# A third pair of k tiles with seven products in place of eight, in a transformer block's large products

## The chip, the core and the metric

The kernel runs on one NeuronCore of a Trainium2 chip. Its engines run side by side, each with its own instruction list, in order: PE (the tensor engine; PEld is its weight load), DVE (vector), ACT (scalar), POOL (GpSimd) and SP (sync, which here only issues transfers). Data lies in HBM, is brought to SBUF by DMA, and PE writes its results to PSUM, eight banks of 128 x 512 float32. The metric is the device time of one execution in microseconds, the median of several runs.

## What is computed

One block of a streaming encoder on 256 tokens with a model width of 2048, in float32:

```python
def mixer_block(u, w_in, lb, hg_norm_w, rel_bias, w_branch_a, w_branch_b, w_out):
    z = u @ w_in
    hq, hf, hi, hg, aq, ak, av, gates = jnp.split(z, SPLIT_POINTS, axis=-1)
    ...
    gate_a, gate_b = jnp.split(jax.nn.sigmoid(gates), 2, axis=-1)
    merged = gate_a * (y_a @ w_branch_a) + gate_b * (y_b @ w_branch_b)
    return merged @ w_out

def reference(x, w_in, lb_logits, hg_norm_w, rel_bias, w_branch_a, w_branch_b, w_out,
              norm_mix_w, norm_mlp_w, w_up, w_down, norm_final_w):
    ...
        h = h + mixer_block(rms_norm(h, norm_mix_w[l]), w_in[l], lb_all[l], hg_norm_w[l],
                            rel_bias[l], w_branch_a[l], w_branch_b[l], w_out[l])
        u = rms_norm(h, norm_mlp_w[l])
        h = h + jnp.square(jax.nn.relu(u @ w_up[l])) @ w_down[l]
    return rms_norm(h, norm_final_w)
```

y_a is a gated linear recurrence, y_b an attention over chunks; both are left as they are. The large products are those with w_in (2048 x 11264), the branches (1024 x 2048 each), w_out (2048 x 2048), w_up (2048 x 8192) and w_down (8192 x 2048).

## The kernel before

**Products in three parts.** Each float32 operand is split into a rounded high part and a rest, `hi` and `lo` (`split`, L88): ACT copies to hi, DVE subtracts to get lo. A product of two 128-row tiles is then three matmuls with 512 columns (`mm3`, L142): hi with hi, hi with lo and lo with hi. The left side (256 tokens, so two row halves m = 0 and 1) is split once and stays in SBUF. The weights are streamed: a piece of 128 x 1024 values (512 KB), two k tiles of 512 columns, is loaded on SP's queue into a `raw` buffer (`piece`, L631) and split into a `wh` and a `wl` buffer (`parts`, L642). There are seven raw buffers and six pairs of wh and wl (`BUFS`, L621). A pool gives out a buffer when its last reader is done.

**Units.** `gemm_s` (L681) computes a unit: 256 rows by 1024 columns, n0 and n1 of 512 each, over 16 k tiles. There are 20 of them in the order ga2, gb0, gb2 (the gates' part of w_in), wo0, wo2 (w_out), then four times up and down: up00, up02, dn00, dn02, up10 and so on to dn30. The last 1024 columns of w_down in the fourth quarter are computed plainly by `gemm2` (L656), with the last four pieces of the last 512 columns held so that row half 0 ends before row half 1. Without savings a unit would have 16 x 2 x 2 = 64 products.

**Seven in place of eight.** A unit takes k tiles in pairs (k, k + 4). Such a pair is a 2 x 2 matrix of left tiles (row half by k tile) times a 2 x 2 matrix of weight tiles (k tile by column half), eight products. For the pairs (0, 4) and (1, 5) Winograd's form of Strassen's scheme is used, which needs seven products with sums on both sides. A product here spans both pairs, so it has 2 x 3 matmuls. `combos` (L586) makes the sums S2, S4, S5, S7 of the left side once for each left side and splits them; it is called seven times (x, m, h, and u in each quarter). The sums on the weight side are made by DVE in the raw buffers, `add` (L692), between the splits: four pieces 11, 22, 12, 21 are loaded, 22 += 12, 12 += 11, 11 += 22, 21 += 11, and each state of a piece is split when its product comes. The seven products p1 to p7 go into the four accumulators c11, c12, c21 and c22 (`bank`, six PSUM banks). c21 starts as ACT's copy of c11 (`copy`, L724); u1 and u2 are copies of c21 at two moments, subtracted in PSUM by DVE (`less`, L735). `fresh` makes PE write a bank once before ACT does, so that PE adds to it afterwards (`seeded`, L729).

**The other six pairs.** `plain` (L715) loads a piece of two neighbouring k tiles of one column half and multiplies it by both row halves, 12 matmuls. Two such pieces (k = 2 for each column half) are put between the seven products, partly as halves, to fill waits; ten follow. When the first column half is complete, `done` takes its banks away (sigmoid, squared relu, or an addition to h1); the last piece of the second half is left over (`late`) and is multiplied inside the next unit by `flush`. `between` is other work set in there: transposes of finished blocks (`turn`, `turns`, `h_blocks`), with their splits and `combos`.

**What sets the order.** The program is written in one sequence, and a scheduler places the instructions of each engine; splits, sums and copies are raised by `high_priority`. Within an engine's list nothing overtakes. Each transfer on SP waits for its raw buffer, in SP's order.

Of the kernel before, what the change touches and what calls it, by code (L numbers as in the profile page):

```python
# [16 lines left out]
P = 128  # L17
T = 256
# [32 lines left out]
def tile_hybrid_block(  # L51
# [36 lines left out]
    def split(hi, lo, src, copy=None):  # L88
        (copy or nc.scalar.copy)(hi, src)  # L89
        nc.vector.tensor_tensor(lo, src, hi.bitcast(F32), op=ALU.subtract)  # L90
# [130 lines left out]
    def rows(factors, what):  # L221

        wide = small.tile([P, NM, P], F32, name=f"wide_{what}", tag="wide", bufs=2)
# [124 lines left out]
    def hgrn_scores(n, kk, b, q):  # L348
# [11 lines left out]
        for i, B in enumerate(LEVELS):  # L360
# [10 lines left out]
            rr = small.tile([P, npar, 4], F32, name=f"rr{n}_{B}", tag=f"rr{B}", bufs=2)  # L371
# [130 lines left out]
    TOK = 18  # L502
# [82 lines left out]

    def combos(lhs, what, home):  # L586

        full = []
        for j in range(2):
            f = tk.tile([P, 2, T], F32, name=f"full_{what}{j}", tag="t", bufs=TOK)  # L590
            nc.vector.tensor_tensor(f, lhs[j][:, :2, 0, :].bitcast(F32), lhs[j][:, :2, 1, :].bitcast(F32), op=ALU.add)
            full.append(f)
        a11, a21 = full[0][:, :, :P], full[0][:, :, P:]
        a12, a22 = full[1][:, :, :P], full[1][:, :, P:]
        made = {}
        s = {i: tk.tile([P, 2, P], F32, name=f"s{i}_{what}", tag="t", bufs=TOK) for i in (5, 2, 4, 7)}
        nc.vector.tensor_tensor(s[5], a21, a22, op=ALU.subtract)
        nc.vector.tensor_tensor(s[2], s[5], a11, op=ALU.subtract)
        nc.vector.tensor_tensor(s[4], a12, s[2], op=ALU.add)
        nc.vector.tensor_tensor(s[7], a11, a21, op=ALU.subtract)  # L600
        for i in (4, 2, 7, 5):
            t = (tk if home == "a" else xp).tile([P, 2, 2, P], F32R, name=f"S{i}_{what}", tag=f"S{i}{home}", bufs=1)
            split(t[:, :, 0, :], t[:, :, 1, :], s[i])
            made[i] = t
        return made
# [15 lines left out]
    BUFS = {"raw": (6, 1), "wh": (4, 2), "wl": (4, 2)}  # L621
# [9 lines left out]
    def piece(w, n0, kt, what):  # L631

        raw = buf("raw", F32, what)
        if w.shape[-1] < NC:
            nb = NC // T
            src = w[n0 // T:n0 // T + nb, kt // 8, :, kt % 8:kt % 8 + 2, :].rearrange("c p a n -> p c a n")
            nc.sync.dma_start(raw.rearrange("p (c a n) -> p c a n", c=nb, n=T), src)
        else:
            nc.sync.dma_start(raw.rearrange("p (a n) -> p a n", n=NC), w[n0 // NC, kt // 4, :, kt % 4:kt % 4 + 2, :])
        return raw  # L640

    def parts(raw, w, what):  # L642

        made = [buf(t, F32R, what) for t in ("wh", "wl")]
        dst, src = made, raw
        if w.shape[-1] < NC:
            dst = [t.rearrange("p (a c n) -> p a c n", a=2, n=T) for t in made]
            src = raw.rearrange("p (c a n) -> p a c n", a=2, n=T)
        with tc.high_priority(offset=2000):
# [6 lines left out]
    def gemm2(lhs, w, n0, nkt, what, kt0=0, tail=0):  # L656

        acc = [bank(f"{what}{m}") for m in range(NM)]
        held = []

        def mm(m, k, wh, wl):
            for a in range(2):
                mm3(acc[m], *lhs_of(lhs, k + a, m), wh[:, a], wl[:, a], k + a == 0, k + a == nkt - 1)

        for k in range(0, nkt, 2):
            ps = (k, *parts(piece(w, n0, kt0 + k, f"{what}{k}"), w, f"{what}{k}"))
            if k >= nkt - tail:
                held.append(ps)
                continue
            for m in range(NM):  # L670
                mm(m, *ps)
        for m in range(NM):
            for ps in held:
                mm(m, *ps)
        return acc
# [5 lines left out]
    def gemm_s(lhs, S, w, n0, what, done, kt0=0, between=None, fresh=()):  # L681
# [6 lines left out]
        B = {}  # L688
        for i, (n, k) in {"11": (n0, 0), "22": (n1, 4), "12": (n1, 0), "21": (n0, 4)}.items():
            B[i] = piece(w, n, kt0 + k, f"{what}{i}")  # L690

        def add(dst, b):  # L692
            with tc.high_priority(offset=2000):
                nc.vector.tensor_tensor(B[dst], B[dst], B[b], op=ALU.add)  # L694

        def product(i, lh, src, n):

            wh, wl = parts(B[src], w, f"{what}{n}")

            def mm():  # L700
                first = i not in c
                if first:
                    c[i] = bank(f"{what}c{i}")
                for a in range(2):
                    mm3(c[i], *lh(a), wh[:, a], wl[:, a], first and a == 0, False)

            return mm
# [7 lines left out]
        def plain(k, n):  # L715
            wh, wl = parts(piece(w, n0 + n * NC, kt0 + k, f"{what}r{n}_{k}"), w, f"{what}r{n}_{k}")

            def mm(m):
                for a in range(2):
                    mm3(c["12"[m] + "12"[n]], *lhs_of(lhs, k + a, m), wh[:, a], wl[:, a], False, k + a == KD - 1)  # L720

            return mm
# [6 lines left out]
        def seeded(i):  # L729

            c[i] = bank(f"{what}c{i}")
            if i in fresh:
                nc.tensor.matmul(c[i], lhs[0][:, 0, 0, 0:P], lhs[0][:, 0].rearrange("p u t -> p (u t)"), start=True, stop=False, skip_group_check=True)

        def less(dst, i, t):  # L735
            with tc.high_priority(offset=2000):
                nc.vector.tensor_tensor(c[dst], c[i], t, op=ALU.subtract)

        p1 = product("11", of(0, 0), "11", "p1")
        p3 = product("12", comb(4), "22", "p3")  # L740
        add("22", "12")
        add("12", "11")
        p1()
        seeded("21")
        copy(c["21"], "11")
        product("22", comb(5), "12", "p5")()
        flush()
        add("11", "22")
        product("21", comb(2), "11", "p6")()
        u1 = copy(token(f"u1_{what}"), "21")  # L750
        seeded("12")
        less("12", "22", u1)
        product("11", of(0, 1), "21", "p2")()
        ps = plain(2, 0)
        ps(0)
        p3()
        product("21", comb(7), "22", "p7")()
        add("21", "11")
        u2 = copy(token(f"u2_{what}"), "21")
        pq = plain(2, 1)  # L760
        pq(0)
        pq(1)
        product("21", of(1, 1), "21", "p4")()
        less("22", "22", u2)
        ps(1)
        if between:
            between()
        def both(n, *ks):
            for k in ks:
                ps = plain(k, n)  # L770
                ps(0)
                ps(1)
# [5 lines left out]
        both(0, 6, 8)  # L778
        both(1, 6, 8)
        both(0, 10, 12, 14)  # L780
        end(0)
        both(1, 10, 12)

        def rest():
            both(1, 14)
            end(1)
# [10 lines left out]
    for gates, c, col, what, fresh in ((ga, 2, C_GA, "ga", ("21", "12")), (gb, 0, C_GB, "gb", ("21",)), (gb, 2, C_GB, "gb", ())):  # L797
# [56 lines left out]
    for n0 in (0, 2):  # L854
# [5 lines left out]
        gemm_s(mT, Sm, w_out, n0 * NC, f"wo{n0}", lambda m, n, acc, n0=n0: evict(h1[n0 + n][m], acc),  # L860
# [7 lines left out]
    for qd in range(NQ):  # L868
# [23 lines left out]
        for c in range(0, 4, 2):  # L892
# [11 lines left out]
            gemm_s(hT, Sh, w_up, qd * (FF // NQ) + c * NC, f"up{qd}{c}", done, between=turns)  # L904
# [26 lines left out]
        for n0 in (0, 2):  # L931
            if not (last and n0):
                gemm_s(uT, Su, w_down, n0 * NC, f"dn{qd}{n0}", lambda m, n, acc, n0=n0: out_of(m, n0 + n, acc), kt0=qd * KD,
                       between=None if n0 else turns)
                continue
# [48 lines left out]
```

## Time and profile before

| | us |
|---|---|
| median of three runs | 1450.09 (1448.04 to 1452.49) |
| the profiled execution, its own time | 1450.73 |
| its span, first to last instruction | 1449.0 |
| mean granted clock of PE | 0.995 of full speed |

In the profile a group of instructions has its line, engine, operation, the tiles written and read, the shape and the count, then busy time, mean ns of one, and the idle time before with what ended it. A row of the timeline begins with start and duration in us. wh_up20p is a buffer of unit up20 for a product p1 to p7, wh_up20r one for a plain piece. A matmul's row lasts longer than the time to the next one's start, as matmuls are pipelined; its cost is read from the starts.

### The profile page before, as it was taken

Reading aid. Unit: us, or ns where it says so; the run is one execution under the profiler, and the core shown is the slowest. Engines: PE = TensorE matmul, PEld = TensorE weight load, DVE = VectorE, ACT = ScalarE, POOL = GpSimd, SP = SyncE. Lnnn points to the kernel's source line nnn. Section 1 sums busy time; section 2 is a strip of 40 time slices with the busy share of each in tenths; the row PEclk is TensorE's granted clock in tenths of the full one; section 3 lists DMA queues with packets and bytes.
Section 4 is the critical chain, followed back from the end, with each engine's and each line's share of the span. In section 5 each row is a group of like instructions: output and inputs, shape, how many; then the busy total and the mean of one; then the engine's idle time right before and its main releaser. Section 6 shows DMA issues by size and latency. Waiting matters only on the chain.

```text
span 1449.0 us, 18212 instructions
## 1 busy us (share of the span) xinstructions
PE 1427.1 (98%) x6741; PEld 1185.2 (82%) x6741; DVE 1047.8 (72%) x1364; ACT 807.3 (56%) x1040; POOL 34.5 (2%) x96
## 2 busy tenths in 40 slices
PE   9999999999999999999999999999999999999997
PEld 7878888888787888888888887888888887888886
DVE  7797978565657774677887876778776868677753
ACT  6755844464555554445666654566545665456642
POOL 2000001010000000000000000000000000000000
PEclk9999999999999999999999999999999999999999
DMA  9644554646456656666655566555557645666551
GB/s 323 218 158 143 161 172 133 195 127 194 143 180 212 216 187 205 195 198 218 204 189 167 170 201 228 190 187 171 183 204 233 203 152 182 216 209 229 196 182 59
DMA packets 106089, 272.87 MB, mean 188 GB/s; under 512 B 8960, under 2 KB 9728, under 8 KB 105616
## 3 DMA queue, kind: packets, MB, share of 16 engines
q1 hardware_dynamic: 103264, 264.80, 55.5%
q0 software_dynamic: 1584, 5.31, 1.4%
q10 hardware_dynamic: 1152, 1.60, 0.3%
q8 instruction: 53, 0.87, 0.2%
q14 instruction: 36, 0.29, 0.1%
HBM read 269.57 MB, written 2.10 MB: 187 GB/s over the span
## 4 chain that ended last, share of the span: by engine, by line
PE 93%; DVE 3%; ACT 2%; issue 1%; DMA 1%; POOL 0%; SPq 0%; POOLq 0%; ACTq 0%
PE acc_hq L171 2%; PE acc_ak L171 2%; PE acc_aq L171 2%; PE acc_hf L171 2%; PE ps L395 1%; PE acc_bb L145 1%; PE acc_bb L143 1%; PE acc_ba L145 1%; PE acc_av L145 1%; PE acc_bb L144 1%; PE acc_ba L144 1%; PE acc_av L143 1%; PE acc_ba L143 1%; PE acc_av L144 1%; PE acc_dn02c L143 1%; PE acc_up22c L143 1%
## 5 line engine op out<-in xcount | busy, mean ns | idle before, releaser
L171 PE MATMUL acc_hf<-act_x,wh_hf 128*128 128x512 f32 x128 | 47.8, 409 | 0.2
L171 PE MATMUL acc_aq<-act_x,wh_aq 128*128 128x512 f32 x128 | 47.9, 407 | 0.0
L171 PE MATMUL acc_hq<-act_x,wh_hq 128*128 128x512 f32 x128 | 45.9, 398 | 0.0
L171 PE MATMUL acc_ak<-act_x,wh_ak 128*128 128x512 f32 x128 | 44.8, 396 | 0.0
L694 DVE TENSOR_TENSOR raw_up<-raw_up,raw_up 128x1024 f32<-128x1024 f32 x32 | 39.2, 1224 | 1.0
L170 PE MATMUL acc_aq<-act_x,wl_aq 128*128 128x256 f32 x120 | 35.2, 294 | 0.0
L694 DVE TENSOR_TENSOR raw_dn<-raw_dn,raw_dn 128x1024 f32<-128x1024 f32 x28 | 34.3, 1224 | 0.9
L170 PE MATMUL acc_hf<-act_x,wl_hf 128*128 128x256 f32 x120 | 34.4, 287 | 0.0
L90 DVE TENSOR_TENSOR wl_ga<-raw_ga,wh_ga 128x1024 fp32r<-128x1024 f32 x16 | 19.6, 1225 | 19.5 <-ACT wh_ga L89 19.5
L170 PE MATMUL acc_ak<-act_x,wl_ak 128*128 128x256 f32 x120 | 33.5, 279 | 0.0
L170 PE MATMUL acc_hq<-act_x,wl_hq 128*128 128x256 f32 x120 | 33.5, 279 | 0.0
L90 DVE TENSOR_TENSOR wl_av<-raw_av,wh_av 128x1024 fp32r<-128x1024 f32 x16 | 19.6, 1225 | 18.1 <-ACT wh_av L89 18.1
L90 DVE TENSOR_TENSOR wl_dn<-raw_dn,wh_dn 128x1024 fp32r<-128x1024 f32 x16 | 19.6, 1226 | 16.7 <-ACT wh_dn L89 16.7
L90 DVE TENSOR_TENSOR wl_ba<-raw_ba,wh_ba 128x1024 fp32r<-128x1024 f32 x16 | 19.6, 1225 | 16.5 <-ACT wh_ba L89 16.3
L90 DVE TENSOR_TENSOR wl_bb<-raw_bb,wh_bb 128x1024 fp32r<-128x1024 f32 x16 | 19.6, 1224 | 16.0 <-ACT wh_bb L89 16.0
L89 ACT CAST wh_bb<-raw_bb 128x1024 fp32r<-128x1024 f32 x16 | 16.9, 1056 | 23.5 <-PE acc_ba L145 12.7
L89 ACT CAST wh_dn<-raw_dn 128x1024 fp32r<-128x1024 f32 x16 | 16.9, 1056 | 23.0 <-PE acc_dn L145 13.3
L89 ACT CAST wh_ba<-raw_ba 128x1024 fp32r<-128x1024 f32 x16 | 16.9, 1055 | 22.6 <-PE acc_ba L145 10.0
L89 ACT CAST wh_av<-raw_av 128x1024 fp32r<-128x1024 f32 x16 | 16.9, 1056 | 22.0 <-PE acc_av L145 12.3
L171 PEld LDWEIGHTS acc_hf<-act_x,wh_hf 128*128 128x128 f32 x128 | 24.3, 190 | 5.6 <-DVE wh_hf L89 0.3
L89 ACT CAST wh_aq<-raw_aq 128x1024 fp32r<-128x1024 f32 x16 | 16.8, 1052 | 21.4 <-PE acc_aq L171 8.1
L171 PEld LDWEIGHTS acc_hq<-act_x,wh_hq 128*128 128x128 f32 x128 | 24.3, 190 | 5.4
(840 smaller groups left out, 5026.2 us busy)
## 6 DMA issues: line engine op xcount, KB each, us to landing
raw_dn<-in_w_down_dram SPq DMA_DIRECT2D x44, 512.0 KB, 5.4
raw_up<-in_w_up_dram SPq DMA_DIRECT2D x32, 512.0 KB, 5.2
raw_ga<-in_w_in_t_dram SPq DMA_DIRECT2D x20, 512.0 KB, 4.5
raw_hi<-in_w_in_n_dram SPq DMA_DIRECT2D x16, 512.0 KB, 4.5
raw_hg<-in_w_in_n_dram SPq DMA_DIRECT2D x16, 512.0 KB, 3.6
raw_aq<-in_w_in_t_dram SPq DMA_DIRECT2D x16, 512.0 KB, 4.4
raw_ak<-in_w_in_t_dram SPq DMA_DIRECT2D x16, 512.0 KB, 4.1
raw_av<-in_w_in_n_dram SPq DMA_DIRECT2D x16, 512.0 KB, 4.2
```

The source lines that it names most:

```text
L89: (copy or nc.scalar.copy)(hi, src)
L90: nc.vector.tensor_tensor(lo, src, hi.bitcast(F32), op=ALU.subtract)
L143: nc.tensor.matmul(acc, hi, wh, start=first, stop=False, skip_group_check=True)
L144: nc.tensor.matmul(acc, hi, wl, start=False, stop=False, skip_group_check=True)
L145: nc.tensor.matmul(acc, lo, wh, start=False, stop=last, skip_group_check=True)
L170: nc.tensor.matmul(acc[:, cb, 0:T], wl[:, c], r[:, 0, :], start=False, stop=False)
L171: nc.tensor.matmul(acc[:, cb, :], wh[:, c], r.rearrange("p u t -> p (u t)"), start=kt == 0, stop=kt == nkt - 1)
L395: nc.tensor.matmul(ps[:, m, :], klf[:, a * P:(a + 1) * P], qrf[:, a * 192:(a + 1) * 192], start=True, stop=True)
L694: nc.vector.tensor_tensor(B[dst], B[dst], B[b], op=ALU.add)
```

## The change

- Three pairs, (0, 4), (1, 5) and (2, 6), are now done with seven products; k tiles 3 and 7 become the first plain piece of each column half. `combos` uses 384 columns in place of 256 and adds hi and lo by row half; S5, S7, S2 and S4 are made in place.
- The third pair's four weight tiles come as two pieces of mixed halves: X holds tiles 11 and 22 of that pair, Y tiles 21 and 12. `piece` takes two halves and issues two transfers of 256 KB where they are not neighbours. The sums on X and Y are made on halves (128 x 512); X is split twice, Y once and its first half once more.
- In wo2 and up00 only two pairs are done so (`r=2`). All other units, and the last one of w_down, which is now a `gemm_s` with `tail`, take three: 18 and that one.
- A split piece is multiplied as soon as its turn comes: p3 is no longer held back, and the two plain pieces with it are used as halves around p7 and p4. Bank 12 now gets p3 directly, and DVE adds a copy of bank 22 (s5) and takes u1 off later.
- Buffers: eight raw in place of seven, 17 tokens (128 x 512) in place of 18, and small tiles of the recurrence moved to another pool.

```diff
 def combos(lhs, what, home):
-    for j in range(2):
-        f = tk.tile([P, 2, T], F32, name=f"full_{what}{j}", tag="t", bufs=TOK)
-        nc.vector.tensor_tensor(f, lhs[j][:, :2, 0, :].bitcast(F32), lhs[j][:, :2, 1, :].bitcast(F32), op=ALU.add)
...
+    for m in range(NM):
+        for j in range(2):
+            t = tk.tile([P, R, P], F32, name=f"a{m}{j}_{what}", tag="t", bufs=TOK)
+            x = lhs[j][:, :R, :, m * P:(m + 1) * P].bitcast(F32)
+            nc.vector.tensor_tensor(t, x[:, :, 0, :], x[:, :, 1, :], op=ALU.add)
...
-    BUFS = {"raw": (6, 1), "wh": (4, 2), "wl": (4, 2)}
+    BUFS = {"raw": (6, 2), "wh": (4, 2), "wl": (4, 2)}
...
+    def piece(w, what, *halves):
+        raw = buf("raw", F32, what)
...
+        for i, (n, k) in enumerate(halves):
+            nc.sync.dma_start(raw[:, i * NC:(i + 1) * NC].rearrange("p (c n) -> p c n", n=ncols),
+                              w[n // ncols:(n + NC) // ncols, k // kpr, :, k % kpr, :].rearrange("c p n -> p c n"))
+        return raw, False
...
+    def gemm_s(lhs, S, w, n0, what, done, r=R, kt0=0, between=None, fresh=False, tail=False):
+        W11 = load("11", (n0, 0), (n0, 1))
+        if r == 3:
+            X = load("x", (n0, 2), (n1, 6))
+        W22 = load("22", (n1, 4), (n1, 5))
+        W12 = load("12", (n1, 0), (n1, 1))
+        if r == 3:
+            Y = load("y", (n0, 6), (n1, 2))
+        W21 = load("21", (n0, 4), (n0, 5))
...
+        p = parts(W11, f"{what}p1")
+        if r == 3:
+            px = parts(X, f"{what}px")
+        mm("11", of(0, 0), p, *both)
+        if r == 3:
+            mm("11", of(0, 0), px, (0, 2))
+        c["21"] = bank(f"{what}c21")
...
+        copy(c["21"], "11")
+        p = parts(W22, f"{what}p3")
+        add(W22[0], W12[0])
+        add(W12[0], W11[0])
+        mm("12", comb(4), p, *both)
+        if r == 3:
+            mm("12", comb(4), px, (1, 2))
+        p = parts(W12, f"{what}p5")
+        mm("22", comb(5), p, *both)
+        if r == 3:
+            add(half(X, 1), half(Y, 1))
+            add(half(Y, 1), half(X, 0))
+            py = parts(Y, f"{what}py")
+            mm("22", comb(5), py, (1, 2))
+        more("12", copy(token(f"s5_{what}"), "22"), ALU.add)
+        if r == 3:
+            mm("11", of(0, 1), py, (0, 2))
+        p = parts(W21, f"{what}p2")
+        mm("11", of(0, 1), p, *both)
+        add(W11[0], W22[0])
+        flush()
+        p = parts(W11, f"{what}p6")
+        mm("21", comb(2), p, *both)
+        if r == 3:
+            add(half(X, 0), half(X, 1))
+            px = parts(X, f"{what}px2")
+            mm("21", comb(2), px, (0, 2))
+        u1 = copy(token(f"u1_{what}"), "21")
...
+        left = [(k, k + 1) for k in range(2, KD, 2) if k != 4] if r == 2 else [(3, 7)] + [(k, k + 1) for k in range(8, KD, 2)]
+        q1 = plain(1, *left[0])
+        q1(1)
+        more("12", u1, ALU.subtract)
+        p = parts(W22, f"{what}p7")
+        mm("21", comb(7), p, *both)
+        if r == 3:
+            mm("21", comb(7), px, (1, 2))
+        u2 = copy(token(f"u2_{what}"), "21")
+        q1(0)
+        add(W21[0], W11[0])
+        q0 = plain(0, *left[0])
+        q0(0)
+        more("22", u2, ALU.subtract)
+        p = parts(W21, f"{what}p4")
+        mm("21", of(1, 1), p, *both)
+        if r == 3:
+            add(half(Y, 0), half(X, 0))
+            mm("21", of(1, 1), parts(Y, f"{what}p4y", 0), (0, 2))
+        q0(1)
...
+        plains(0, *left[1:-3])
+        plains(1, *left[1:-3])
+        plains(0, *left[-3:])
+        end(0)
+        if tail:
+            held = [plain(1, *ks) for ks in left[-3:]]
+            for m in range(NM):
+                for p in held:
+                    p(m)
+                done(m, 1, c["12"[m] + "2"])
+            return
+        plains(1, *left[-3:-1])
...
-    gemm_s(hT, Sh, w_up, qd * (FF // NQ) + c * NC, f"up{qd}{c}", done, between=turns)
+    gemm_s(hT, Sh, w_up, qd * (FF // NQ) + c * NC, f"up{qd}{c}", done, r=R if qd or c else 2, between=turns)
...
     for n0 in (0, 2):
-        if not (last and n0):
-            gemm_s(uT, Su, w_down, n0 * NC, f"dn{qd}{n0}", lambda m, n, acc, n0=n0: out_of(m, n0 + n, acc), kt0=qd * KD,
-                   between=None if n0 else turns)
-            continue
-        flush()
-        for n in (2, 3):
-            for m, acc in enumerate(gemm2(uT, w_down, n * NC, KD, f"dn{qd}{n}", kt0=qd * KD, tail=8 if n == 3 else 0)):
-                out_of(m, n, acc)
+        gemm_s(uT, Su, w_down, n0 * NC, f"dn{qd}{n0}", lambda m, n, acc, n0=n0: out_of(m, n0 + n, acc), kt0=qd * KD,
+               between=None if n0 else turns, tail=last and n0 == 2)
```

`mm(i, lh, ps, *tiles)` multiplies the named tiles of a split piece into bank i, three matmuls each; `more` adds to or subtracts from a bank in PSUM on DVE; `half(W, i)` is one 512-column half of a raw piece; `plain(n, *ks)` loads and splits a plain piece and returns a function that multiplies it by one row half.

More of the change, by code (lines that the diff above doesn't have):

```diff
@@ L679, in evict, with add, mm @@
             nc.vector.tensor_tensor(dst, acc, dst, op=ALU.add)
-    def gemm_s(lhs, S, w, n0, what, done, kt0=0, between=None, fresh=()):
+    def gemm_s(lhs, S, w, n0, what, done, r=R, kt0=0, between=None, fresh=False, tail=False):
         n1 = n0 + NC
         c = {}
[L688 to L692, printed above, removed]
-            with tc.high_priority(offset=2000):
[L694 to L707, printed above, removed]
+        load = lambda name, *halves: piece(w, f"{what}{name}", *[(n, kt0 + k) for n, k in halves])
+        W11 = load("11", (n0, 0), (n0, 1))
[6 more added lines that the diff above has]
+        W21 = load("21", (n0, 4), (n0, 5))
+        def add(dst, t):
+            with tc.high_priority(offset=2000):
+                nc.vector.tensor_tensor(dst, dst, t, op=ALU.add)
+        half = lambda W, i: W[0][:, i * NC:(i + 1) * NC]
+        def mm(i, lh, ps, *tiles):
+            first = i not in c
+            if first:
+                c[i] = bank(f"{what}c{i}")
+            wh, wl = ps
+            for a, k in tiles:
+                mm3(c[i], *lh(k), wh[:, a], wl[:, a], first, False)
+                first = False
         def of(m, jj):
@@ L713, in comb @@
             return lambda k: [S[i][:, k, u, :] for u in range(2)]
[L715 to L722, printed above, removed]
+        both = ((0, 0), (1, 1))
         def copy(dst, i):
@@ L759, in gemm_s, with more @@
-        u2 = copy(token(f"u2_{what}"), "21")
[L760 to L765, printed above, removed]
+        def more(i, t, op):
+            with tc.high_priority(offset=2000):
+                nc.vector.tensor_tensor(c[i], c[i], t, op=op)
+        p = parts(W11, f"{what}p1")
[4 more added lines that the diff above has]
+            mm("11", of(0, 0), px, (0, 2))
```

123 lines of the change are left out of this document (50 added, 73 removed).

## The prediction

> **What bounds the kernel now.** I read the page first, then the waits of PE (the tensor engine), then its timeline, then the windows of four units in a row.
>
> ```profile
> span 1449.0 us, 18212 instructions
> PE 1427.1 (98%) x6741; PEld 1185.2 (82%) x6741; DVE 1047.8 (72%) x1364; ACT 807.3 (56%) x1040; POOL 34.5 (2%) x96
> PEclk9999999999999999999999999999999999999999
> PE 93%; DVE 3%; ACT 2%; issue 1%; DMA 1%; POOL 0%; SPq 0%; POOLq 0%; ACTq 0%
> ```
>
> PE is busy for 98% of the span at full granted clock, and the chain that ended last is 93% PE. What PE lost in waiting is little:
>
> ```profile
> PE ps L395 <- DVE sd L357: 3.3, 3, 2.9
> PE acc_dn02c L143 <- ACT wh_dn02r L89: 1.8, 1, 1.8
> PE acc_ga2c L143 <- ACT acc_ga2c L726: 0.6, 1, 0.6
> PE acc_dn20c L143 <- ACT act_u L89: 0.5, 1, 0.5
> ```
>
> Only about 3 us of it lie in the units that change. So a matmul that is left out is worth its spacing, as long as the others still come without a gap. The spacing is read from starts, because the 0.39 us of a row overlaps the next one. Between these two rows of PE's timeline lie 72 steps:
>
> ```profile
> 899.79 0.39 PE L145 MATMUL acc_dn02c<-wh_dn02r,act_u 128*128 128x512 f32 x1
> 916.12 0.39 PE L145 MATMUL acc_dn02c<-wh_dn02r,act_u 128*128 128x512 f32 x1
> ```
>
> (916.12 − 899.79) / 72 = 0.2268 us. A unit of 186 matmuls takes 42.2 us. The windows show how full the others are meanwhile (columns: length, PE, PEld, DVE, ACT, POOL, PE's clock, DMA share, GB/s; the four are up20, up22, dn20 and dn22):
>
> ```profile
> 1089.00:1131.00 42.00, 42.00 (x187) 34.75 (x186) 30.00 (x27) 23.52 (x26) 0.00 (x0) 1.00 0.63 205
> 1131.00:1175.00 44.00, 44.00 (x202) 36.18 (x201) 35.20 (x40) 29.11 (x38) 0.00 (x0) 1.00 0.59 190
> 1175.00:1221.00 46.00, 45.49 (x206) 36.43 (x205) 32.65 (x32) 25.45 (x30) 0.00 (x0) 1.00 0.57 182
> 1221.00:1263.00 42.00, 42.00 (x187) 34.75 (x187) 30.89 (x29) 21.32 (x22) 0.58 (x1) 1.00 0.58 198
> ```
>
> DVE (vector) has 9 to 13 us free in a unit, ACT (scalar) 15 or more, and the DMA engines are busy 0.6 of the time (the last share of a row).
>
> **The change part by part.** *Matmuls.* A product is three matmuls. One product less in 18 units is 54; w_down's last unit goes from two plain halves to the seven-product form and loses three products, 9; of the three seeding matmuls at ga2 and gb0 two remain, 1. That is 64, and the two instruction lists differ by just that number. 64 × 0.2268 = 14.5 us off PE. The Trainium skill, TensorE: Matmul & The Clock Gate, section "Wait — 56ns, not 53.3ns?", measures 215.7 ns between warm matmuls of 512 columns; by that the term would be 13.8 us; here the measured spacing is 226.8 ns, and it decides.
>
> *Work added on DVE and ACT.* Prices:
>
> ```profile
> L694 DVE TENSOR_TENSOR raw_up<-raw_up,raw_up 128x1024 f32<-128x1024 f32 x32 | 39.2, 1224 | 1.0
> L90 DVE TENSOR_TENSOR wl_up20r<-raw_up20r,wh_up20r 128x1024 fp32r<-128x1024 f32 x12 | 14.7, 1224 | 6.9 <-ACT wh_up20r L89 6.7
> L591 DVE TENSOR_TENSOR full_u<-act_u x8: 691/693/693, 805.3 to 1328.9; 128x512 f32<-128x512 f32 x8
> L90 DVE TENSOR_TENSOR S_u<-s_u,S_u x16: 416/418/421, 811.9 to 1335.6; 128x256 fp32r<-128x256 f32 x16
> L737 DVE TENSOR_TENSOR acc_up20c<-acc_up20c,u_up x2: 696/698/700, 1097.4 to 1104.2; 128x512 f32<-128x512 f32 x2
> L89 ACT CAST wh_up20r<-raw_up20r 128x1024 fp32r<-128x1024 f32 x12 | 12.7, 1056 | 8.4 <-PE acc_up20c L145 8.4
> L726 ACT COPY u_up<-acc_up20c x2: 590/590/590, 1096.0 to 1101.5; 128x512 f32<-128x512 f32 x2
> ```
>
> A changed unit gets 1.5 more splits (px, py and a second px come in place of two plain ones, and the half split p4y), four half adds and one more correction of a bank (s5). On DVE: 1.5 × 1.22 + 4 × 0.69 + 0.70 = 5.3 us; on ACT: 1.5 × 1.06 + 0.59 = 2.2 us. The combinations of the left side grow from 256 to 384 columns; no row has that shape on DVE, so it lies between 0.42 and 0.69, and I take the middle, 0.56: about 2 us for each of the seven. up20 comes to 35 of 41.5 us, up22 to 42.5 of 43.3. Recorded times overlap, though:
>
> ```profile
> 1085.43 1.22 DVE L90 TENSOR_TENSOR wl_up20p<-raw_up,wh_up20p 128x1024 fp32r<-128x1024 f32 x1
> 1086.57 1.22 DVE L90 TENSOR_TENSOR wl_dn12r<-raw_dn12r,wh_dn12r 128x1024 fp32r<-128x1024 f32 x1
> 1122.86 3.74 DVE L694 TENSOR_TENSOR raw_up<-raw_up,raw_up 128x1024 f32<-128x1024 f32 x3
> ```
>
> Splits in a row start 1.14 us apart; adds that need each other take 3.74 / 3 = 1.25. So DVE's real need in up22 is some 38 us. On the mean it is hidden behind PE; the question is the burst. The seven products with their plain companions are 99 matmuls, 22.5 us of PE, and DVE has about 28 us of work for them, 4 us of it evictions and corrections. The missing 6 us have to be done ahead, and six split buffers allow that: the plain part leaves DVE 2.7 − 1.1 = 1.6 us per piece.
>
> I laid out one unit by hand, up20, with t = 0 where PE begins p1, in the order in which the changed kernel's lists stand. PE wants p6 after 48 matmuls, t = 10.9; p7 after 63, t = 14.3; bank 12 again (first use of the (3,7) piece there) after 72, t = 16.3. DVE can start p3's split at −5.7: its buffer falls free three plain pieces before t = 0, at −8.2, ACT's copy and one eviction follow. From p3 to p6 it has six splits, four full adds and an eviction, 6 × 1.14 + 4 × 1.25 + 0.6 = 12.4, so p6 is ready at 6.7: 4 us early. Then come the two tight places:
>
> 1. ACT copies bank 21 (u1) between p6 and p7. Before, 18 matmuls (4.1 us) lay between them; now only the 6 of one half of the (3,7) piece, 1.36 us. The copy in the trace starts 0.2 to 0.3 us behind PE and takes 0.59: done 0.8 to 0.9 after p6, 0.5 us to spare, if ACT is free.
> 2. ACT is in order, and ahead of that copy stand the copies for the second (3,7) piece and for p4. That piece's transfer can start only when p6's split has freed its raw buffer, t = 6.7, as two transfers of 256 KB. How long transfers take (two views, of tiles loaded by w_up and by w_down):
>
> ```profile
> 1096.03 0.59 ACT L726 COPY u_up<-acc_up20c 128x512 f32<-128x512 f32 x1 [0.26 <-PE acc_up20c L145]
> 1096.52 1.06 ACT L89 CAST wh_up20p<-raw_up 128x1024 fp32r<-128x1024 f32 x1
> 1097.47 1.05 ACT L89 CAST wh_up20r<-raw_up20r 128x1024 fp32r<-128x1024 f32 x1
> DMA to landing us min/median/max: 3.7/4.7/5.3
> DMA to landing us min/median/max: 3.5/4.6/6.3
> ```
>
> It lands at 6.7 + 3.7 to 4.7 = 10.4 to 11.4; two ACT copies 0.95 apart and u1 end at 13.7 (u1 by PE) to 13.9; wanted 14.3. DVE then has the (3,7) split, an eviction, p4 and the correction of bank 12: ready at 15.2 to 16.1, wanted 16.3. So nothing to half a microsecond is left, and units that carry more before p6 (dn20 with the combinations of u, wo2 and up00 with those of h) will miss it. Bounds per unit: 0 at a landing of 3.7; at 6.3, 13.0 + 1.9 + 0.6 − 14.3 = 1.2 us late. I take 0.15, near the median's end, as not every unit is late: 19 × 0.15 = 3 us.
>
> *Transfers.* 76 loads of 512 KB become 152 of 256 KB, the same bytes, all on SP's queue, which only issues; X and Y stand there ahead of W22 and W21 and wait for older buffers, but all four are wanted more than 5 us after landing. One more raw buffer, one token less, and the factor tiles in another pool: nothing, no load or copy of the hand layout waits for them; without that cover one copy of 0.6 us.
>
> *The end.* The two row halves of the last bank are now 18 matmuls apart, 4.1 us, where it was 24.
>
> ```profile
> 1434.44 0.69 DVE L679 TENSOR_TENSOR h<-acc_dn,h 128x512 f32<-128x512 f32 x1 [8.52 <-PE acc_dn L145]
> 1436.98 1.34 ACT L928 ACTIVATE h<-h,rstd 128x512 f32<-128x512 f32 x2 [1.08 <-POOL rstd L96]
> ```
>
> The first half's chain lasts 1438.32 − 1434.44 = 3.9 us, so it still ends before the second needs ACT: 0, at most 0.5.
>
> **Sum.** 1449.0 − 14.5 + 3 = 1437.5 of span. That execution took 1450.73, 1.7 more than its span and 0.6 above the median of 1450.09. So 1439.2 for its like, and 1438.6 as a median. The old waits in ga2, dn02 and dn20 may go too (−3), which I leave to the range.
>
> **The rivals.**
> - *Bursts on DVE decide.* If its lead shrinks below what the hand layout shows, PE waits for splits in the units with turns and combinations, eleven of the 21. For it: up22's need of 38 to 42.5 us in 43.3. Against: the same units ran before at 35.2 of 44 with no wait. At 1 us each: 1438.6 + 11 = 1450.
> - *The second (3,7) transfer lands late; slower.* The place is p7 waiting for u1 behind ACT's copy of that piece. It decides from 14.5 / 19 = 0.76 us per unit on, a landing of 5.9 us. For it: the maxima of 5.3 and 6.3 above, and that the piece shares the queue with two others issued in the 5 us before it. Against: the median of 4.7. At a whole 7 us, the price is 13.7 + 2.5 − 14.3 = 1.9 a unit, 36 us, 1472; at 6.1, 1.0 a unit, 1455. By DMA: Bandwidth & Descriptors of the Trainium skill, section "Anatomy of one DMA", a transfer costs some 2.0 us plus its bytes at 436 GB/s, an estimate of 2.6 for each half and 5.2 if the halves followed each other, where the whole one would need 3.2; at 5.2 a unit would be 0.1 late. The shortest landing here of a whole one is 3.5.
> - *The change saves nothing on PE*, because the matmuls left out are made up by others: excluded by the lists but for a slip of mine; 1450.
>
> **How the numbers follow.** Forecast 0.63: 1438.6, own range 1434 to 1445. DVE bursts 0.16: 1446 to 1453. Late transfer 0.18: 1450 to 1470, mostly near 1456. No saving 0.03. The range reaches from 1433.5 (all waits gone, 14.5 + 2 off) to 1455. What a measurement can tell from no change is 0.3%, 4.4 us: faster means below 1445.7, slower above 1454.5. Faster: 0.62 of the first, 0.04 of the second, 0.02 of the third: 0.68. Slower: 0.03 and 0.13: 0.16 and a little for what I do not see, 0.19. Same: 0.13.
>
> **What would show it.** PE should have 64 matmuls fewer at 0.2268 us and still 98%; DVE some 1170 us busy, ACT some 860. In the waits of PE, a line with p7's bank 21 waiting for ACT's u, or bank 12 for DVE's correction, totals under 5 us if I am right and over 14 if the second rival is; waits for wl tiles would be the first. A higher spacing of the matmuls, or waits at places that I did not lay out (gates, w_out), would make me wrong in another way.

## The result, and the profile after

| | before | after |
|---|---|---|
| median, us | 1449.8 (4 runs) | 1461.63 (1460.13 to 1462.88, 4 runs) |
| ratio to before | | 1.008, 95% interval 1.0061 to 1.0098 |
| span of the profiled execution | 1449.0 | 1460.1 |
| span less PE's busy time | 21.9 | 24.4 |

The forecast was 1438.6 with 1455 as the upper end; the change made the kernel slower, by 0.8%. The page of the kernel after:

```profile
span 1460.1 us, 18523 instructions
...
PE 1435.7 (98%) x6677; PEld 1175.4 (81%) x6677; DVE 1151.5 (79%) x1522; ACT 847.3 (58%) x1105; POOL 34.7 (2%) x96
...
PEclk9999999999999999999999999999999999999999
...
PE 81%; DVE 8%; DMA 4%; ACT 3%; issue 2%; SPq 0%; POOL 0%; POOLq 0%; ACTq 0%; DVEq 0%
```

PE executes the 64 matmuls fewer that were counted, 6677 against 6741, at full granted clock, and yet it is busy 8.6 us longer. So the loss isn't in waits first of all. The waits of PE in the units (engine and tile, who released it, us in total, times, the longest):

```profile
PE acc_gb0c L143 <- ACT u_gb L726: 1.6, 1, 1.6
PE acc_ga2c L143 <- ACT wh_ga2p L89: 1.4, 1, 1.4
...
PE acc_dn20c L143 <- ACT u_dn L726: 0.9, 1, 0.9
PE acc_dn32c L143 <- ACT u_dn L726: 0.8, 1, 0.8
...
PE acc_dn10c L143 <- ACT u_dn L726: 0.5, 1, 0.5
PE acc_dn30c L143 <- ACT u_dn L726: 0.4, 1, 0.4
```

The copy u holds PE up for 4.2 us in all, where the "late transfer" rival needed over 14; span less busy grew by only 2.5. What grew is the step from one matmul to the next. Two rows of PE's timeline, 72 steps apart in the plain part of the same unit as in the prediction:

```profile
904.61 0.39 PE L143 MATMUL acc_dn02c<-wh_dn02r,act_u 128*128 128x512 f32 x1
...
921.34 0.39 PE L143 MATMUL acc_dn02c<-wh_dn02r,act_u 128*128 128x512 f32 x1
```

(921.34 − 904.61) / 72 = 0.2324 us, where it was 0.2268. The step grew in stages that the change doesn't touch, too. Here are rows of the branch products 72 steps apart, first of the kernel before, then of the kernel after:

```profile
565.43 0.39 PE L143 MATMUL acc_ba<-wh_ba,act_ya 128*128 128x512 f32 x1
...
581.75 0.39 PE L143 MATMUL acc_bb<-wh_bb,act_yb 128*128 128x512 f32 x1
```

```profile
571.39 0.39 PE L143 MATMUL acc_ba<-wh_ba,act_ya 128*128 128x512 f32 x1
...
588.11 0.40 PE L143 MATMUL acc_bb<-wh_bb,act_yb 128*128 128x512 f32 x1
```

That is 0.2267 us before and 0.2322 after, in code that is the same in both. Rows of unit up20 show that it isn't so for all matmuls. The operands behind the arrow are the moving weight tile and the stationary left tile; S_h is a combination, act_h a plain left tile:

```profile
1110.02 0.39 PE L143 MATMUL acc_up20c<-wh_up20p,S_h 128*128 128x512 f32 x1
...
1111.83 0.40 PE L145 MATMUL acc_up20c<-wh_up20px,S_h 128*128 128x512 f32 x1
...
1115.51 0.40 PE L143 MATMUL acc_up20c<-wh_up20r,act_h 128*128 128x512 f32 x1
...
1118.07 0.39 PE L145 MATMUL acc_up20c<-wh_up20r,act_h 128*128 128x512 f32 x1
```

Eight steps with S take 1.81 us, 0.2263 each; eleven with act take 2.56, 0.2327 each. Shape, type, clock and the pools of the moving buffers are the same.

The compiled kernels' addresses give the difference. The tiles of the pool small lie ahead of the weight buffers in SBUF. With the factor tiles wide and rr gone from it, the weight buffers behind it moved down by 4736 bytes per partition, 18 × 256 + 128:

| first byte modulo 256 | act | wh, wl | S |
|---|---|---|---|
| before | 0 | 0 | 0 |
| after | 0 | 128 | 128 |

wh and S moved together, act stayed. Theory A is that this placement costs some 5 ns a matmul. Theory B, the rival, is that the new order of the work does it: denser work of DVE and ACT, or the smaller transfers. The branch products already speak against B, as their work is the same in both kernels.

### The profile page after: what moved, and what is told of

Same layout as the page of the kernel before. It is cut to its first block, busy times and chain, and to the rows that moved or that the text cites. A ratio compares the mean times of both kernels' runs of the same rounds, so it can differ in the third digit from the quotient of the medians.

```text
span 1460.1 us, 18523 instructions
## 1 busy us (share of the span) xinstructions
PE 1435.7 (98%) x6677; PEld 1175.4 (81%) x6677; DVE 1151.5 (79%) x1522; ACT 847.3 (58%) x1105; POOL 34.7 (2%) x96
## 4 chain that ended last, share of the span: by engine, by line
PE 81%; DVE 8%; DMA 4%; ACT 3%; issue 2%; SPq 0%; POOL 0%; POOLq 0%; ACTq 0%; DVEq 0%
PE acc_ak L171 2%; PE acc_hq L171 2%; PE acc_aq L171 2%; PE acc_hf L171 1%; DVE raw_dn L702 1%; PE ps L395 1%; PE acc_av L143 1%; PE acc_bb L143 1%; PE acc_bb L144 1%; PE acc_ba L145 1%; PE acc_bb L145 1%; PE acc_av L145 1%; PE acc_ba L143 1%; PE acc_av L144 1%; PE acc_ba L144 1%
## 5 line engine op out<-in xcount | busy, mean ns | idle before, releaser
L171 PE MATMUL acc_aq<-act_x,wh_aq 128*128 128x512 f32 x128 | 48.0, 406 | 0.0
L171 PE MATMUL acc_hf<-act_x,wh_hf 128*128 128x512 f32 x128 | 47.2, 403 | 0.7 <-DVE wh_hf L89 0.7
L171 PE MATMUL acc_hq<-act_x,wh_hq 128*128 128x512 f32 x128 | 45.7, 394 | 0.0
L171 PE MATMUL acc_ak<-act_x,wh_ak 128*128 128x512 f32 x128 | 45.0, 394 | 0.0
L702 DVE TENSOR_TENSOR raw_dn<-raw_dn,raw_dn 128x1024 f32<-128x1024 f32 x32 | 39.0, 1218 | 0.2
L89 ACT CAST wh_ga<-raw_ga 128x1024 fp32r<-128x1024 f32 x16 | 16.8, 1049 | 21.4 <-PE acc_ga L145 12.6
L171 PEld LDWEIGHTS acc_hf<-act_x,wh_hf 128*128 128x128 f32 x128 | 24.1, 188 | 5.8 <-DVE wh_hf L89 0.9
L89 ACT CAST wh_hg<-raw_hg 128x1024 fp32r<-128x1024 f32 x16 | 16.7, 1046 | 20.6 <-PE acc_hg L145 13.8
L171 PEld LDWEIGHTS acc_hq<-act_x,wh_hq 128*128 128x128 f32 x128 | 24.0, 188 | 5.3
```

What stands on the lines that cost most here:

```text
L171: nc.tensor.matmul(acc[:, cb, :], wh[:, c], r.rearrange("p u t -> p (u t)"), start=kt == 0, stop=kt == nkt - 1)
L702: nc.vector.tensor_tensor(dst, dst, t, op=ALU.add)
```

## The experiments

**1. Placement undone.** A tile that nobody reads, `room`, is made 128 bytes longer; no instruction is added, only the one that fills `room` writes more.

```diff
-    room = small.tile([P, 8], F32, name="room", tag="room", bufs=1)
+    room = small.tile([P, 40], F32, name="room", tag="room", bufs=1)
```

> The changed kernel with one edit: a small unused tile is 160 bytes per partition long in place of 32, which pushes every buffer behind it up by 128 bytes. No instruction is added or taken away; the raw, wh and wl buffers then start at multiples of 256 bytes again, as in the kernel before, not at odd multiples of 128. Theory A (placement: the pool moves of wide and rr shifted wh and wl by 4736 bytes, and a matmul whose moving operand starts off a multiple of 256 bytes takes about 5 ns more): spacing of the matmuls back from 231.4 to 226.8 ns, PE busy about 1410 us, time 1433 to 1437 us, about 15 us under the kernel before. Theory B (the new order: DVE's and ACT's denser work, or the smaller transfers, slow the matmuls): spacing stays at 231 ns, time stays 1460 to 1463 us.

Measured: 1442.67 us, 0.9941 of before (0.9924 to 0.9958). The page, and two rows of PE's timeline 72 steps apart in dn02:

```profile
span 1442.7 us, 18523 instructions
...
PE 1413.3 (98%) x6677; PEld 1172.0 (81%) x6677; DVE 1148.4 (80%) x1522; ACT 848.1 (59%) x1105; POOL 34.3 (2%) x96
```

```profile
895.68 0.39 PE L143 MATMUL acc_dn02c<-wh_dn02r,act_u 128*128 128x512 f32 x1
...
912.00 0.39 PE L143 MATMUL acc_dn02c<-wh_dn02r,act_u 128*128 128x512 f32 x1
```

16.32 / 72 = 0.2267 us: the spacing is back, and PE's busy time falls by 22.4 us with the work of DVE and ACT unchanged. Theory B falls. But the time stays 6 to 10 us over what A alone gave: span less busy is 29.4, 7.5 over before. (The profiled execution was the slowest of the four, 1.8 us over their median.) Experiments 7, 8 and 11 take that up.

**2. The same edit in the kernel before** (`room` from 8 to 40 columns), where it spoils the placement.

> The kernel before with the same one edit (the unused tile 160 bytes in place of 32): its raw, wh and wl buffers move from multiples of 256 bytes to odd multiples of 128, and nothing else changes. Theory A (placement): spacing of the unit matmuls from 226.7 to about 231.5 ns, some 5000 matmuls by 5.2 ns = 26 us, time 1474 to 1478 us. Theory B (the new order): no change, 1448 to 1452 us.

Measured: 1473.74 us, 1.0166 (1.0151 to 1.0181), just under A's range. The page:

```profile
span 1474.5 us, 18212 instructions
...
PE 1452.0 (98%) x6741; PEld 1187.7 (81%) x6741; DVE 1050.3 (71%) x1364; ACT 804.1 (55%) x1040; POOL 34.3 (2%) x96
```

An unread 128 bytes cost the old kernel 24.9 us of PE, without any of the new order.

**3. Six raw buffers left where they were.** The kernel after, with 128 bytes of gap in the weight pool between its six raw buffers and wh. wh, wl and everything behind them, S and the other two raw buffers too, go to multiples of 256.

```diff
+                if t == "raw" and not gap:
+                    gap.append(wpool.tile([P, 32], F32, name="gap", tag="gap", bufs=1))
+                    nc.gpsimd.memset(gap[0], 0.0)
```

> The changed kernel with a gap of 128 bytes between the six raw buffers and the wh and wl buffers of the same pool: these six raw buffers stay at odd multiples of 128 bytes, wh and wl go to multiples of 256. Theory A1 (it is the start of the matmuls' moving operand): as fast as with everything moved, 1433 to 1437 us. Theory A2 (it is the start of the transfers' destination, or of what DVE and ACT read): as slow as the changed kernel, 1458 to 1463 us. Theory B (the new order): 1460 to 1463 us.

Measured: 1441.72 us, 0.9942 (0.9926 to 0.9958), as in experiment 1 and like it above A1's range. PE's row:

```profile
PE 1412.8 (98%) x6677; PEld 1172.8 (81%) x6677; DVE 1148.7 (80%) x1522; ACT 846.3 (59%) x1105; POOL 34.8 (2%) x97
```

Six raw buffers, into which DMA writes and from which ACT and DVE read, still lay at 128 modulo 256, and PE is as fast. So their start is not what counts.

**4. One part of the change alone**: the kernel before with the two pool moves.

```diff
-        wide = small.tile([P, NM, P], F32, name=f"wide_{what}", tag="wide", bufs=2)
+        wide = hp.tile([P, NM, P], F32, name=f"wide_{what}", tag="wide", bufs=1)
...
-            rr = small.tile([P, npar, 4], F32, name=f"rr{n}_{B}", tag=f"rr{B}", bufs=2)
+            rr = hp.tile([P, npar, 4], F32, name=f"rr{n}_{B}", tag=f"rr{B}", bufs=2)
```

> The kernel before with one part of the change alone: the tiles wide and rr are taken from the pool hp (wide with one buffer), in place of the pool small. All products, transfers and splits stay as before. Theory A (placement): everything behind the small pool moves down by 4736 bytes, wh and wl to odd multiples of 128, and the time goes to 1474 to 1478 us. Theory C (of the move only the one buffer of wide counts: a copy of 0.6 us per set of factors without cover): at most 2 us, 1450 to 1452 us. Theory B: 1450 us.

Measured: 1475.05 us, 1.0171 (1.0156 to 1.0186). PE's row:

```profile
PE 1453.3 (99%) x6741; PEld 1188.6 (81%) x6741; DVE 1050.3 (71%) x1364; ACT 804.9 (55%) x1040; POOL 34.5 (2%) x96
```

Two lines that move factor tiles slow the old kernel by 25 us, all of it in PE's busy time (26.2 us). Experiment 2, which keeps both buffers of wide, is within its interval: no cost of the single buffer is to be seen.

**5 and 6. Absolute or relative.** In the kernel after, a constant tile ahead of act is made longer by 128 bytes, which moves act to 128 and wh, wl and S on to 0; in 6 `room` as well, so that all lie at 128.

```diff
-    mhalf = const.tile([P, 32], F32, name="mhalf")
+    mhalf = const.tile([P, 64], F32, name="mhalf")
```

> The changed kernel with one edit: a constant tile ahead of all others is 128 bytes per partition longer (only its first columns are used). The left tiles (act) move to odd multiples of 128 bytes, and wh, wl and the combinations S, which lie at odd multiples in the changed kernel, to multiples of 256. Theory A-absolute (a matmul is slow when its moving operand starts off a multiple of 256): fast, like the kernel with wh and wl put back, 1440 to 1444 us, spacing 226.8 ns. Theory A-relative (a matmul is slow when its moving operand and the stationary operand that is loaded meanwhile lie differently modulo 256; the changed kernel's trace shows 227 ns for most products with S on the left and 232 for those with act): products with act stay slow, products with S stay at 227, time 1458 to 1463 us.

> The changed kernel with both tiles longer, the constant one by 128 bytes and the unused one by 128: act, wh, wl and S all lie at odd multiples of 128 bytes. Theory A-absolute: as slow as the changed kernel, 1458 to 1463 us. Theory A-relative: all pairs lie alike, spacing 226.8 ns, 1440 to 1444 us.

Measured: 1460.99 us for 5, 1.0082 (1.0062 to 1.0102); 1446.12 for 6, 0.9967 (0.9955 to 0.998). PE's rows on the pages of 5 and 6:

```profile
PE 1433.4 (98%) x6677; PEld 1174.7 (80%) x6677; DVE 1151.9 (79%) x1522; ACT 846.6 (58%) x1105; POOL 34.7 (2%) x96
```

```profile
PE 1414.6 (98%) x6677; PEld 1173.3 (81%) x6677; DVE 1148.9 (79%) x1522; ACT 848.1 (59%) x1105; POOL 34.5 (2%) x96
```

With wh at a multiple of 256 and act off it, PE is slow; with both off it, it is fast. So it isn't the moving operand's own address: it is how moving and stationary tiles lie to each other. Products with S, which moved with wh, fit that: over the whole trace of the kernel after, the median step behind a matmul with S is 227 ns and behind one with act 232. Two things limit the rule. In every run whose step is back at 0.227 us the distance from act to wh, wl and S is a multiple of 512 bytes, and no run has them 256 apart, so "alike modulo 256" may as well be "modulo 512". And products with S aren't always untouched: in experiment 2, where they stand six or twelve in a row between products with act, their median step is 231 ns although S and wh lie alike. Experiment 6 is 2 us over what was expected of it and 3.5 over experiment 1; of the 2.6 between the two spans 1.3 are PE's busy time and 1.3 waits, and why the waits differ was not followed up.

**9 and 10. Smaller offsets**: the kernel before with `room` at 16 columns (32 bytes more) and at 24 (64 more).

> The kernel before with the unused tile 64 bytes long in place of 32: wh, wl and S lie 32 bytes off the left tiles modulo 256, where 128 bytes cost 24.2 us in the second experiment. Theory G (any difference modulo 256 costs the same): 1473 to 1476 us. Theory H (only the upper half of a 256-byte stretch against the lower half collides): 1449 to 1452 us. Theory I (a finer grain counts too, a start off a multiple of 64 bytes costs more): above 1476 us.

> The kernel before with the unused tile 96 bytes long in place of 32: wh, wl and S lie 64 bytes off the left tiles modulo 256. Theory G (any difference modulo 256): 1473 to 1476 us. Theory H (only halves of 256 bytes): 1449 to 1452 us. Theory I (only starts off multiples of 64 bytes cost more): not above 1476 us.

Measured: 1477.41 us for 32 bytes, 1.0187 (1.0172 to 1.0202); 1460.21 for 64, 1.0071 (1.0056 to 1.0086). PE's rows on the pages of 9 and 10:

```profile
PE 1454.7 (99%) x6741; PEld 1183.6 (80%) x6741; DVE 1050.4 (71%) x1364; ACT 804.4 (55%) x1040; POOL 34.6 (2%) x96
```

```profile
PE 1437.2 (99%) x6741; PEld 1186.3 (81%) x6741; DVE 1049.3 (72%) x1364; ACT 804.8 (55%) x1040; POOL 34.0 (2%) x96
```

An offset of 32 bytes costs PE 27.6 us, 64 bytes 10.1, 128 bytes 24.9. G wanted all alike, H wanted 32 and 64 free, and both miss. Theory I, that a start off a multiple of 64 costs more, holds within its bounds (above 1476 and not above 1476 us), but they were wide, and it doesn't say why 64 costs less than half of 128. The cost depends on the offset and isn't monotonic. Of other offsets none was tried, and what collides inside the chip stays open.

**7. p2 behind p6.** Now to the 7.5 us of waits that were left. ACT's timeline around the longest of them, in dn20 of experiment 1, and PE's rows around it:

```profile
1183.89 1.05 ACT L89 CAST wh_dn20r<-raw_dn20r 128x1024 fp32r<-128x1024 f32 x1 [3.36 <-DMA raw_dn20r<-in_w_down_dram]
1184.85 1.26 ACT L944 ACTIVATE r<-acc_up22c,rstd 128x512 f32<-128x512 f32 x2
1186.00 1.04 ACT L89 CAST wh_dn20p<-raw_dn 128x1024 fp32r<-128x1024 f32 x1
1186.93 0.63 ACT L89 CAST wh_dn20p4y<-raw_dn20y 128x512 fp32r<-128x512 f32 x1
1187.45 0.60 ACT L726 COPY u_dn<-acc_dn20c 128x512 f32<-128x512 f32 x1
```

```profile
1185.10 0.39 PE L145 MATMUL acc_dn20c<-wh_dn20px,S_u 128*128 128x512 f32 x1
...
1186.46 0.39 PE L145 MATMUL acc_dn20c<-wh_dn20r,act_u 128*128 128x512 f32 x1
1188.10 0.50 PE L143 MATMUL acc_dn20c<-wh_dn20p,S_u 128*128 128x512 f32 x1 [1.25 <-ACT u_dn L726]
```

p6 begins its last matmul at 1185.10, and u1 could start 0.4 us later. ACT comes to it at 1187.45: it sat idle for 3.36 us at the copy of the second (3,7) piece, whose transfer had not landed, and then made that copy, two evictions of the unit before (L944) and p4's two copies. Theory D took the work in front of u1 for the cause, E the end of p6. In 7 the matmuls of p2 go behind p6, which also makes the scheduler put u1 ahead of the second (3,7) copy.

```diff
-        p = parts(W21, f"{what}p2")
-        mm("11", of(0, 1), p, *both)
+        p2 = parts(W21, f"{what}p2")
         add(W11[0], W22[0])
...
         u1 = copy(token(f"u1_{what}"), "21")
+        mm("11", of(0, 1), p2, *both)
```

> The changed kernel with wh and wl at multiples of 256 (the first experiment's edit, 1442.7 us), and the six matmuls of p2 put behind p6, so that 12 matmuls, 2.7 us, cover the copy u1 in place of 6. The first experiment lost 25.9 us in gaps between matmuls against 18.1 before, all of it in front of p7 in units whose predecessor leaves two evictions on ACT. Theory D (u1 comes late because ACT is in order and has two evictions and p4's two casts in front of it): the same casts stay in front of u1, and p7 comes at the same time as before, so the gap shrinks only by what ACT's order changes: u1 is now ahead of the second (3,7) cast, 1 us earlier, gaps down by 4 to 7 us, time 1436 to 1439 us. Theory E (u1 is late because it starts only after p6): also 2.7 us cover, gaps down to 18 us, 1435 us. Theory F (the gaps come from late splits on DVE): no change, 1441 to 1444 us.

Measured: 1432.85 us, 0.9884 (0.987 to 0.9897), faster than both kernels and under what D and E gave. The page, and ACT's timeline at the same place:

```profile
span 1430.9 us, 18489 instructions
...
PE 1410.8 (99%) x6677; PEld 1174.0 (82%) x6677; DVE 1148.5 (80%) x1522; ACT 852.0 (60%) x1105; POOL 34.6 (2%) x96
```

```profile
1175.16 1.04 ACT L89 CAST wh_dn20p<-raw_dn 128x1024 fp32r<-128x1024 f32 x1
1176.10 0.62 ACT L89 CAST wh_dn20p4y<-raw_dn20y 128x512 fp32r<-128x512 f32 x1
1176.62 0.59 ACT L726 COPY u_dn<-acc_dn20c 128x512 f32<-128x512 f32 x1
1177.10 0.64 ACT L945 ACTIVATE r<-r 128x512 f32<-128x512 f32 x1
1177.98 1.06 ACT L89 CAST wh_dn20r<-raw_dn20r 128x1024 fp32r<-128x1024 f32 x1 [0.24 <-PE acc_dn20c L145]
```

The second (3,7) copy now stands behind u1, and span less busy falls to 20.1. p4's two copies are still in front and harm nothing. The edit changed two things, the place in ACT's list and the cover behind p6, and no run takes them apart. By the rows the place should have been enough, which no run shows: u1 lasts 0.59, and the old cover was 1.36.

**8. p4's copies off ACT**, on GpSimd, with u1 where it was.

```diff
-        p = parts(W21, f"{what}p4")
+        p = parts(W21, f"{what}p4", cast=nc.gpsimd.tensor_copy)
...
-            mm("21", of(1, 1), parts(Y, f"{what}p4y", 0), (0, 2))
+            mm("21", of(1, 1), parts(Y, f"{what}p4y", 0, cast=nc.gpsimd.tensor_copy), (0, 2))
```

> The first experiment's kernel with p4's two casts to wh on GpSimd in place of ACT. Theory D (u1 is behind p4's two casts on ACT): 1.6 us of ACT work leave the queue in front of u1, the gaps of up to 1.4 us in front of p7 go, gaps down to 18 to 20 us, time 1435 to 1438 us, if GpSimd makes the casts in under 4 us. Theory E (u1 starts late because p6 ends late): no change, 1441 to 1444 us. If GpSimd is slower than that or slows DVE, p4 comes late and the time goes over 1444 us.

Measured: 1442.99 us, 0.9951 (0.9938 to 0.9963), no gain on experiment 1. Its profiled execution shows the waits for u smaller (0.8 us at most in dn00) and a new one, of PE for DVE's split of u ahead of a transpose:

```profile
PE tp_u L106 <- DVE act_u L90: 3.1, 1, 3.1
...
PE acc_dn00c L143 <- ACT u_dn L726: 0.8, 1, 0.8
```

Over all units the waits for u fall from 7.7 us in experiment 1 to 4.3, and the new wait takes back nearly all of it. So D's p4 copies are a part of the lateness, not the whole: in dn20 ACT still sits idle for 3.21 us at the second (3,7) copy.

**11. Two pairs in the new order**: experiment 1's kernel with `R = 2`.

> The first experiment's kernel (wh and wl at multiples of 256, 1442.7 us) with two pairs of k tiles in all units in place of three: 19 units get one product more, 57 matmuls, 57 x 0.2268 = 12.9 us of PE; the half transfers and the half split go, the new order stays. Theory A with the sum of the prediction: PE's matmuls cost 12.9 us more, and with gaps between 18 us (as before the change) and 25.9 us (as in the first experiment) the time is 1447 to 1456 us. Theory D (ACT's queue in front of u1): p4's half cast is gone and the plain piece comes in one transfer, so the gaps fall to 18 to 22 us, 1447 to 1452 us. If the third pair saves nothing: 1442 us.

Measured: 1444.52 us, 0.9962 (0.9947 to 0.9977), under the range that either theory gave. The page:

```profile
span 1443.9 us, 18247 instructions
...
PE 1423.1 (99%) x6734; PEld 1183.9 (82%) x6734; DVE 1069.5 (74%) x1408; ACT 818.8 (57%) x1067; POOL 34.1 (2%) x96
```

Span less busy is 20.8, no more than before the change: without the third pair no cost of u1's place in the list is to be seen. So the third pair's 57 matmuls are worth 1444.52 − 1442.67 = 1.9 us as the change orders them, which the overlapping intervals of the two runs do not tell from nothing. With u1 in time it is 1444.52 − 1432.85 = 11.7 us, close to the 12.9 of the spacing; two pairs with p2 behind p6 were not run.

**12. Three pairs in all 21 units**: experiment 7's kernel with `r=R` in wo2 and up00 too.

> The kernel with p2 behind p6 (1432.85 us) with three pairs in all 21 units, where wo2 and up00 had two: 6 matmuls less, 1.4 us. If the splits of these two units, which carry the combinations of h and the transposes, keep up: 1431.0 to 1432.0 us. If DVE is late there: 1 to 4 us of gaps in wo2 and up00, 1432.5 to 1436 us.

Measured: 1437.11 us, 0.991 (0.9894 to 0.9927), 4.3 over experiment 7 and above both ranges. PE waits in up00 for the combinations of h:

```profile
PE acc_up00c L143 <- ACT S_h L89: 2.3, 1, 2.3
```

That is 2.3 of the 4.3 us; the rest was not followed up. The two exceptions of the change are worth keeping together; which of the two counts was not tried.

## Why the prediction was wrong, step by step

- **The failed step** is a sentence of the part on transfers: "the factor tiles in another pool: nothing, no load or copy of the hand layout waits for them; without that cover one copy of 0.6 us". It priced what the tiles' readers wait for and not where the tiles behind them come to lie. Measured alone (experiment 4) it costs 25 us in the kernel before; in the kernel after it is 22.4 us of PE's busy time (experiment 1). The sum put it at nothing, and its upper end of 1455 came from waits. With the placement undone, the time of experiment 1, 1442.67 us, lies 4.1 over the forecast of 1438.6.
- **Matmuls: right.** 64 fewer at 0.2268 is 14.5; with the placement undone PE's busy time is 13.8 to 16.3 under before (experiments 1, 3 and 7, which run the same matmuls). The assumption hidden in the term, that the spacing stays, is what the pool move broke. "A higher spacing of the matmuls" stood last among the things that would make the forecast wrong, without a chance or a price.
- **Work on DVE and ACT: right.** DVE 1151.5 us busy (some 1170 said), ACT 847.3 (860). In the kernel after PE's waits in the units are for ACT's copies, not for DVE's splits, so the rival of DVE's bursts did not happen.
- **The hand layout: right place, wrong size, hidden in the result.** u1 on ACT behind the second (3,7) piece was named as the tight place and priced at 3 us. The kernel after shows 2.5 us more of span less busy than before; at the old spacing it is 7.5. The slow matmuls hide a part: in runs of the change's order span less busy is 24.4 and 25.9 where they are slow (after, experiment 5) and 29.3 to 30.7 where they are fast (experiments 1, 3 and 6). The lines of experiment 1 in which PE waits for u, eight in all, add up to 7.7 us; these are the two longest:

```profile
PE acc_gb0c L143 <- ACT u_gb L726: 1.8, 1, 1.8
...
PE acc_dn20c L143 <- ACT u_dn L726: 1.3, 1, 1.3
```

  Two things were left out of the layout: ACT's two evictions of the unit before, 1.26 us, and p4's half copy, 0.63, both in front of u1. It put 1.9 us between the start of the second (3,7) copy and the start of u1; in dn20 it is 1187.45 − 1183.89 = 3.56. The piece's two transfers were put at 3.7 to 4.7 us to landing. The two of 256 KB in dn20 of experiment 1 took a median of 4.1 each, but the copy needs both, and it started at 1183.89, 5.0 us after the first was issued (the issues on SP, then the transfers issued from 1170 to 1186 us with count, size and median to landing):

```profile
1178.87 1.48 SPq L648 DMA_DIRECT2D raw_dn20r<-in_w_down_dram  x2
```

```profile
raw_dn20r<-in_w_down_dram SPq DMA_DIRECT2D x5, 512.0 KB, 5.2
raw_dn20r<-in_w_down_dram SPq DMA_DIRECT2D x2, 256.0 KB, 4.1
```

  By DMA: Bandwidth & Descriptors of the Trainium skill, section "Anatomy of one DMA — SWDGE (gpsimd) path", the estimate was 2.6 us for a half alone and 5.2 for two in turn. The 5.0 us of the pair are near the second, with other loads in flight; the section's fit is for transfers that GpSimd issues, and these are issued on SP's queue.

- **The rival of the late transfer** forecast 1450 to 1470, and the time lies there, but for another reason: its sign was over 14 us of waits at p7, and 4.2 were found.
- **The end: right.** From the start of the last matmul to the end of the span it is 9.5 us in both kernels.
- **The account.** Span before 1449.0; matmuls −13.8; placement +22.4; waits +2.5. That is 1460.1, the span after.

## What to carry to other kernels

A change that allocates differently moves every buffer behind it. Compare how the addresses of the matmuls' moving and stationary operands lie to each other before pricing such an edit at nothing (wherever the step was 0.227 us here, the distance was a multiple of 512 bytes), and read the matmul spacing in code that the change doesn't touch: if it differs there, as in the branch products here, the new order is a poor suspect. When a copy becomes the only cover between two products, list everything that stands in front of it on its in-order engine, with what the first of them waits for; here, moving one product by a few places was worth 10 us, where the third pair without it brought 1.9, within the noise.

## What the runs showed of the hardware

A matmul of the form 128*128 128x512 f32 with a weight tile moving and a left tile stationary costs 0.2268 us from start to start when the two start alike modulo 256 bytes, at 0 (before) or at 128 (experiment 6), and some 5 ns more when they lie 128 bytes apart, whichever of the two is off (after, experiment 5). Over the kernel's matmuls of this kind that is 22 to 25 us of PE's busy time, some 1.6%; 32 bytes cost 27.6 and 64 bytes 10.1. Wherever the step was 0.227 us, the distance was in fact a multiple of 512 bytes; 256 was not tried.

It is not a rule for every product. In the 512 matmuls of hq, hf, aq and ak with 512 columns (L171), which alternate with ones of 256 columns, the left tile moves and the weight tile is stationary. There the median step is 233 ns in the kernel before, where the tiles lie alike, and 233 in the kernel after, where they lie 128 apart.

The start of six raw buffers, which only DMA, ACT and DVE touch, made no difference (experiment 3).
